# A decoder trunk's opening in a fixed order, its norm weight read from PSUM, and the memory's values ahead of the memory queries

## The chip, the cores and the metric

The kernel runs on one core of a Trainium2 chip. The metric is the device time of one execution in microseconds (us); less is better. Times are compared as medians of repeated runs. One further execution is recorded by the hardware profiler, and all profile lines below come from such executions.

## The reference

The reference computes two layers on a sequence of 512 tokens with 1024 channels, in float32. With `swiglu(t) = (silu(t @ w_gate) * (t @ w_up)) @ w_down`, each layer is

```python
f = swiglu(rmsnorm(h, ffn1_pre_g[l]), ffn1 weights)
h = h + 0.5 * rmsnorm(f, ffn1_post_g[l])
u = rmsnorm(h, mix_pre_g[l])
q_sb, k_sb, v_sb, q_fx, k_fx, v_fx, f_logit, q_mem = split(u @ w_in[l])
o_sb  = stick_breaking_attention(q_sb, k_sb, v_sb)        # 8 heads of 64
o_fx  = forgetting_attention(q_fx, k_fx, v_fx, log_f)     # 8 heads of 64
k_mem, v_mem = split(rmsnorm(mem, mem_norm_g) @ w_mem_kv[l])
o_mem = softmax_attention(q_mem, k_mem, v_mem)            # 4 heads of 128, 256 memory rows
g_sb, g_fx, g_mem = split(sigmoid(u @ w_gate[l] + b_gate[l]))
merged = g_sb * (o_sb @ w_br_sb[l]) + g_fx * (o_fx @ w_br_fox[l]) + g_mem * (o_mem @ w_br_mem[l])
h = h + rmsnorm(merged @ w_out[l], mix_post_g[l])
f = swiglu(rmsnorm(h, ffn2_pre_g[l]), ffn2 weights)
h = h + 0.5 * rmsnorm(f, ffn2_post_g[l])
```

`rmsnorm(t, g)` divides each row by the root of its mean square (plus 1e-6) and multiplies by the weight `g`. The hidden width of `swiglu` is 2816.

## The kernel before

Every float32 matrix is split into a high and a low half in a format that TensorE multiplies in one pass. A product of two matrices is three products of halves: high by high, high by low, low by high (`mm3`, lines 187 to 190). ScalarE makes the high half by a cast (L165, or L168 with a scale), VectorE the low half by subtracting the high one (L166, L169).

The 512 tokens stand in four tiles of 128 rows, `hT[0]` to `hT[3]`. A class `Sub` stands for each norm between two blocks. For one tile it squares and sums the row (`squared`, L520), makes the reciprocal root (`rstd`, L467 to L475), scales the row by it and by the norm's weight (`normed`, L553, into `fs`), transposes the tile on TensorE (`turned`, L563, eight transposes of 128 by 128, into PSUM tiles `ut...`) and splits the result (L168, L169) into `us`. `us[0]` holds channels 0 to 511 and `us[1]` the rest.

Work on TensorE is a queue of jobs, `Q`. A job has weight units, each 128 rows by four or eight, of 512 KB. `fetch` (L236) loads a unit on SyncE's DMA queue into one of two `raw` buffers, and `load` splits it into `wh` and `wl` buffers. `Q.fetch_ahead` issues the next units as soon as a `raw` buffer is counted free. `Q.weave` takes products from the queue one at a time and puts the steps of other chains between them: a chain yields `("wait", us)`, and goes on once that much estimated TensorE time has been recorded. A scheduler underneath may still move an instruction of an engine ahead of others, by its own estimate of when operands are ready; `tc.keep_in_program_order` forbids that for one instruction.

Three places matter here.

*The opening.* `begin()` loads the four tiles of x and the first norm's weight. The weight is one row; `gains(quick=True)` spreads it over 128 partitions by a product with a column of ones (L510, into the PSUM tiles `gqx`) and copies both halves into SBUF (L511). The tiles 0 and 1 are then normed and transposed, and the first two weight units split. These are the units of the first gate tile (`ga`); the first up tile's units (`ua`) are next in the same two `raw` buffers.

*Halves.* In each `ffn` the first gate and up tile are computed for tokens 0 to 255 first and then for tokens 256 to 511 (`halved`), so that the first 96 products need only two tiles. In the opening, tiles 2 and 3 are transposed while the first half runs. Products are issued by `gemm`: one output tile after another, and for each group of 128 channels the three products of halves together. `pga` and `pua` are the gate and up outputs in PSUM of the first block of a layer, `pgc` and `puc` those of its last.

*Entry to the mixing.* While the last tiles of the block before are normed and transposed (`uta`), TensorE works on what doesn't need them: the memory's keys (`pmk`) and the first of two blocks of its values (`pmv_0`). Then come the first block of memory queries (`pqm`, which needs all four tiles), the second block of values, and the second block of queries. The four memory heads follow: scores (`zm`), a softmax on VectorE and ScalarE, transposes (`ptm`), the product with the values (`pvm`), woven with the remaining projections. Between the two, SyncE stores each finished tile of h (`hsave`, L1243), behind which later weight loads on that queue wait.

```python
for c in range(2):
    un = wpair(w_in[l], ND, 3080 + c * 256, f"qm{l}_{c}")
    marks["qm", c] = Q.add(un, lambda c=c, un=un: q_mem(c, un), src.ready(range(NT)) if c == 0 else None)
    if c == 0:
        marks["values"] = rest()
```

`rest()` adds the second block of values. The wait ahead of a tile's transposes is `W_U[t] + self.slack`, with a slack of 4.0 for the norm in front of the mixing.

## Time and profile before

| | |
|---|---|
| median of 3 runs | 2448.37 us (2446.9 to 2449.66) |
| profiled execution, time | 2446.09 us |
| profiled execution, span | 2444.1 us |
| TensorE (PE) busy | 2428.7 us, 99% of the span, 12158 products |
| VectorE (DVE) busy | 1546.0 us, 63% |
| ScalarE (ACT) busy | 1175.3 us, 48% |
| weight and activation loads | 272.20 MB read, 114 GB/s over the span |

A timeline row gives the start, the duration, the engine, the line, the operation, what it writes and reads, the shape and how many instructions were merged into it; in brackets stands the idle time of the engine before it and what ended that. A row of the waits gives the instruction that waited, what it waited for, the total in us, how often, and the longest. A window's row gives its length and then, for each engine shown, busy time and number of instructions, the granted TensorE clock, the share of the DMA engines and GB/s. In a row of grouped instructions stand the busy time and the mean duration in ns. A product's duration reaches past the start of the next one, so the pace is read from the distance between starts.

### The profile page before, as it was taken

What the parts mean: (1) busy time and instruction counts of PE and PEld (TensorE: products, weight loads), DVE (VectorE), ACT (ScalarE), POOL (GpSimd) and SP (SyncE); (2) the same over time, 40 slices, a digit from 0 to 9 for tenths busy, and PEclk for the clock granted to TensorE, in tenths of its full rate; (3) what the DMA queues carried; (4) which work ended last, traced back from release to release, by engine and by line L of the source; (5) the groups of instructions that cost most, each with busy time, mean ns of one, the idle gap of its engine ahead of it and who ended that gap; (6) DMA issues with size and microseconds to landing.
All of it is one profiled execution on the core that took longest, in us unless ns stands there. A gap on an engine that the chain in (4) does not pass through costs nothing.

```text
span 2444.1 us, 30901 instructions
## 1 busy us (share of the span) xinstructions
PE 2428.7 (99%) x12158; PEld 2062.1 (84%) x12158; DVE 1546.0 (63%) x2182; ACT 1175.3 (48%) x1895; POOL 72.6 (3%) x129
## 2 busy tenths in 40 slices
PE   8999999999999999999999999999999999999998
PEld 7888889888888888888888888888888888888887
DVE  4464677677876653656644546876788866445466
ACT  4333365577655543433433333555676655333333
POOL 0000000001110000000000000000011100000000
PEclk9999999999999999999999999999999999999999
DMA  4334344222223433333424343442232243333433
GB/s 138 113 129 129 126 167 147 78 74 74 83 65 114 145 104 108 125 125 128 162 87 131 111 142 133 163 131 70 70 94 71 70 138 129 95 129 104 145 114 129
DMA packets 238597, 280.50 MB, mean 115 GB/s; under 512 B 8666, under 2 KB 188914, under 8 KB 238452
## 3 DMA queue, kind: packets, MB, share of 16 engines
q1 hardware_dynamic: 238356, 278.50, 35.5%
q8 instruction: 95, 1.56, 0.3%
q14 instruction: 50, 0.41, 0.0%
q0 software_dynamic: 96, 0.03, 0.0%
HBM read 272.20 MB, written 6.29 MB: 114 GB/s over the span
## 4 chain that ended last, share of the span: by engine, by line
PE 95%; DVE 2%; ACT 2%; DMA 1%; issue 1%; SPq 0%; DVEq 0%; ACTq 0%
PE pg L188 4%; PE pg L189 4%; PE pg L190 4%; PE pgc L188 3%; PE pga L188 3%; PE pgc L189 3%; PE pga L189 3%; PE puc L188 3%; PE puc L189 3%; PE pgc L190 3%; PE puc L190 3%; PE pga L190 3%; PE pua L188 3%; PE pua L190 3%; PE pua L189 3%; PE pdc L188 3%
## 5 line engine op out<-in xcount | busy, mean ns | idle before, releaser
L188 PE MATMUL pg<-us_a,wh_wg 128*128 128x512 f32 x384 | 150.7, 392 | 0.0
L189 PE MATMUL pg<-us_a,wh_wg 128*128 128x512 f32 x384 | 149.8, 390 | 0.0
L190 PE MATMUL pg<-us_a,wl_wg 128*128 128x512 f32 x384 | 149.6, 390 | 0.0
L190 PE MATMUL puc<-us_b,wl_uc 128*128 128x512 f32 (+1 forms) x384 | 142.5, 371 | 0.0
L189 PE MATMUL puc<-us_b,wh_uc 128*128 128x512 f32 (+1 forms) x384 | 142.5, 371 | 0.0
L188 PE MATMUL puc<-us_b,wh_uc 128*128 128x512 f32 (+1 forms) x384 | 142.4, 372 | 0.0
L188 PE MATMUL pgc<-us_b,wh_gc 128*128 128x512 f32 x320 | 124.5, 389 | 0.0
L189 PE MATMUL pgc<-us_b,wh_gc 128*128 128x512 f32 x320 | 124.5, 389 | 0.0
L190 PE MATMUL pgc<-us_b,wl_gc 128*128 128x512 f32 x320 | 124.5, 389 | 0.0
L166 DVE TENSOR_TENSOR wl_uc<-raw_uc,wh_uc 128x1024 fp32r<-128x1024 f32 x44 | 53.9, 1226 | 107.8 <-ACT wh_uc L165 107.8
L166 DVE TENSOR_TENSOR wl_ua<-raw_ua,wh_ua 128x1024 fp32r<-128x1024 f32 x44 | 53.9, 1226 | 100.8 <-ACT wh_ua L165 100.8
L165 ACT CAST wh_uc<-raw_uc 128x1024 fp32r<-128x1024 f32 x44 | 46.2, 1051 | 92.5 <-PE pgc L189 39.4
L166 DVE TENSOR_TENSOR wl_gc<-raw_gc,wh_gc 128x1024 fp32r<-128x1024 f32 x40 | 48.8, 1224 | 62.7 <-ACT wh_gc L165 62.4
L166 DVE TENSOR_TENSOR wl_ga<-raw_ga,wh_ga 128x1024 fp32r<-128x1024 f32 x40 | 48.8, 1224 | 62.3 <-ACT wh_ga L165 62.1
L165 ACT CAST wh_ua<-raw_ua 128x1024 fp32r<-128x1024 f32 x44 | 46.2, 1050 | 86.2 <-PE pga L189 34.1
L188 PE MATMUL pdc<-wh_dc,ahc 128*128 128x512 f32 x224 | 87.2, 389 | 0.0
L189 PE MATMUL pdc<-wl_dc,ahc 128*128 128x512 f32 x224 | 87.2, 389 | 0.0
L189 PE MATMUL pda<-wl_da,aha 128*128 128x512 f32 x224 | 87.2, 389 | 0.0
L190 PE MATMUL pda<-wh_da,ala 128*128 128x512 f32 x224 | 87.2, 389 | 0.0
L188 PE MATMUL pda<-wh_da,aha 128*128 128x512 f32 x224 | 87.2, 389 | 0.0
L190 PE MATMUL pdc<-wh_dc,alc 128*128 128x512 f32 x224 | 87.1, 389 | 0.0
L190 PEld LDWEIGHTS pg<-us_a,wl_wg 128*128 128x128 f32 x384 | 72.1, 188 | 15.1
(442 smaller groups left out, 7264.3 us busy)
## 6 DMA issues: line engine op xcount, KB each, us to landing
raw_da<-in_ffn_w_down_dram SPq DMA_DIRECT2D x58, 512.0 KB, 3.3
raw_dc<-in_ffn_w_down_dram SPq DMA_DIRECT2D x58, 512.0 KB, 3.2
raw_wg<-in_w_gate_dram SPq DMA_DIRECT2D x48, 512.0 KB, 3.5
raw_ga<-in_ffn_w_gate_dram SPq DMA_DIRECT2D x44, 512.0 KB, 3.6
raw_ua<-in_ffn_w_up_dram SPq DMA_DIRECT2D x44, 512.0 KB, 3.6
raw_gc<-in_ffn_w_gate_dram SPq DMA_DIRECT2D x44, 512.0 KB, 3.6
raw_uc<-in_ffn_w_up_dram SPq DMA_DIRECT2D x44, 512.0 KB, 3.6
raw_wo<-in_w_out_dram SPq DMA_DIRECT2D x24, 512.0 KB, 3.3
```

The costliest lines, as they stand in the source:

```text
L165: both = (nc.scalar.copy(h_ap, src), nc.vector.tensor_tensor(l_ap, src, h_ap.bitcast(F32), ALU.subtract))
L166: nc.vector.tensor_tensor(l_ap, src, h_ap.bitcast(F32), ALU.subtract))
L188: nc.tensor.matmul(pt, lh, rh, start=start, stop=False, skip_group_check=free)
L189: nc.tensor.matmul(pt, lh, rl, start=False, stop=False, skip_group_check=free)
L190: nc.tensor.matmul(pt, ll, rh, start=False, stop=stop, skip_group_check=free)
```

## The change

1. *Opening.* The order of ScalarE's and VectorE's instructions in `begin()` is fixed by dependencies without a semaphore (`in_order`). The spread weight stays in PSUM for the scaling of tiles 0 to 2, which reads it there; ScalarE copies it to SBUF later, for tile 3. Nine products of zeros (`warm`) are put on TensorE, six ahead of the weight's spreading and three between the transposes of tiles 0 and 1. The raw tiles of the first up units come from the pool `v` instead of the two `raw` buffers, and are loaded ahead of the last tile of x. The low halves of tiles 0 and 1 and of the first weights are made after both tiles are scaled. The waits before the transposes of tiles 2 and 3 become 6.5 and 3.2.
2. *Halves.* In every `halved`, the products of high by high of all channels and both output tiles come first, then the products with a low half.
3. *Mixing.* The second block of the memory's values is added to the queue ahead of both blocks of queries, and the slack in front of the mixing becomes 6.0.

```diff
         nc.gpsimd.tensor_scalar(nbfor[:], bfor[:], -1.0, None, ALU.mult)
 
 
+    @contextmanager
+    def in_order(*engines):
+
+        traced = nc.cur_bb.bb.instructions
+        mark = traced[-1]
+        yield
+        traced = nc.cur_bb.bb.instructions
+        at = next(k for k in reversed(range(len(traced))) if traced[k] is mark or traced[k].name == mark.name) + 1
+        nosync = mybir.DependencyInfo(mybir.DependencyClass.NoSync, mybir.DependencyReason.DATA)
+        for e in engines:
+            prev = next((i for i in reversed(traced[:at]) if i.engine == e.engine), None)
+            for i in traced[at:]:
+                if i.engine == e.engine:
+                    if prev is not None:
+                        tc.add_manual_dep(i, prev.name, nosync, reason="in_order")
+                    prev = i
+
     HALVES = (slice(0, S // 2), slice(S // 2, S))
     FULL = slice(0, S)
 
-    def split(h_ap, l_ap, src, scale=None):
+    def split(h_ap, l_ap, src, scale=None, later=False):
 
         if scale is None:
-            both = (nc.scalar.copy(h_ap, src),
-                    nc.vector.tensor_tensor(l_ap, src, h_ap.bitcast(F32), ALU.subtract))
+            both = [nc.scalar.copy(h_ap, src)]
+            make = lambda: nc.vector.tensor_tensor(l_ap, src, h_ap.bitcast(F32), ALU.subtract)
         else:
-            both = (nc.scalar.activation(h_ap, src, AF.Copy, scale=scale),
-                    nc.vector.scalar_tensor_tensor(l_ap, src, scale, h_ap.bitcast(F32), ALU.mult, ALU.subtract))
+            both = [nc.scalar.activation(h_ap, src, AF.Copy, scale=scale)]
+            make = lambda: nc.vector.scalar_tensor_tensor(l_ap, src, scale, h_ap.bitcast(F32), ALU.mult, ALU.subtract)
+        if later:
+            return make
+        both.append(make())
         if Q.pinned:
             for ins in both:
                 tc.keep_in_program_order(ins)
...
 
 
         def __init__(self, src, k0, nk, c0, ncol, name, scale=None):
-            self.tags = ("wh", "wl")
+            self.tags, self.place = ("wh", "wl"), "raw"
             self.src, self.k0, self.nk, self.c0, self.ncol, self.name, self.scale = src, k0, nk, c0, ncol, name, scale
             self.h = self.raw = None
 
...
 
         def ring(self):
 
-            return True
+            return self.place == "raw"
 
         def fetch(self):
             if not self.waits():
                 return
-            Q.fetched += 1
-            self.raw = stile([P, self.nk, self.ncol], "raw", "raw_" + self.name, F32)
+            Q.fetched += self.ring()
+            self.raw = stile([P, self.nk, self.ncol], self.place, "raw_" + self.name, F32)
             nc.sync.dma_start(self.raw[:], self.src[self.k0 * P:(self.k0 + self.nk) * P, self.c0:self.c0 + self.ncol]
                               .rearrange("(k p) c -> p k c", p=P))
 
...
                 return
             self.fetch()
             self.split_from(self.raw[:])
+            self.loaded()
+
+        def loaded(self):
             self.raw = None
-            Q.fetched -= 1
+            if self.ring():
+                Q.fetched -= 1
             Q.fetch_ahead()
 
-        def split_from(self, raw):
+        def split_from(self, raw, **how):
             shape = [P, self.nk, self.ncol]
             if isinstance(self.tags, str):
                 both = stile([P, 2] + shape[1:], self.tags, "w_" + self.name)
...
             else:
                 self.h = stile(shape, self.tags[0], "wh_" + self.name)[:]
                 self.l = stile(shape, self.tags[1], "wl_" + self.name)[:]
-            split(self.h, self.l, raw, scale=self.scale)
+            return split(self.h, self.l, raw, scale=self.scale, **how)
 
     class BlockUnit(Unit):
 
...
                 for row, c in zip(rows, HF):
                     nc.sync.dma_start(row, gain_srcs[i][l:l + 1, c])
                 self.gq = stile([P, D], self.tag, "gq" + self.name, F32)
-                for hf, c in enumerate(HF):
-                    pt = pbank("mm", f"gq{self.name}_{hf}")
-                    nc.tensor.matmul(pt[:], ones, rows[hf], start=True, stop=True)
-                    nc.vector.tensor_copy(self.gq[:, c], pt[:])
+                self.spread = [pbank("mm", f"gq{self.name}_{hf}") for hf in range(2)]
+                for pt, row in zip(self.spread, rows):
+                    tc.keep_in_program_order(nc.tensor.matmul(pt[:], ones, row, start=True, stop=True))
             if self.g_post is not None:
                 self.gp = gain_row(*self.g_post, self.tag, "gp" + self.name)
             if self.g_pre is not None and not quick:
...
                 Q.load_ahead()
                 Q.pinned = False
             c = HALVES[half]
-            for i, pt in enumerate(st["p"]):
-                yield from gemm(pt[:, c], (ug, uu)[i // 2], i % 2, lambda k: act(k, c))
+
+            for uns, pts in ((ug, st["p"][:2]), (uu, st["p"][2:])):
+                for low in (False, True):
+                    for un in uns:
+                        for k, (m, pt) in itertools.product(range(un.nk), enumerate(pts)):
+                            kk, cols = un.k0 + k, slice(m * P, (m + 1) * P)
+                            wh, wl = un.h[:, k, cols], un.l[:, k, cols]
+                            ah, al = act(kk, c)
+                            if low:
+                                nc.tensor.matmul(pt[:, c], wh, al, start=False, stop=False, skip_group_check=True)
+                                nc.tensor.matmul(pt[:, c], wl, ah, start=False, stop=kk == ND - 1, skip_group_check=True)
+                            else:
+                                nc.tensor.matmul(pt[:, c], wh, ah, start=kk == 0, stop=False, skip_group_check=True)
+                            yield (1 + low) * S // 2 * PE_US
             if half == 1:
                 for m in range(2):
                     hidden(f + m, st["p"][m], st["p"][2 + m])
...
             marks["gates", br] = Q.add(ug, lambda: (us_ for m in range(2) for us_ in sigmoid(m)))
             return Q.add(ub, run)
 
+        marks["values"] = rest()
         for c in range(2):
             un = wpair(w_in[l], ND, 3080 + c * 256, f"qm{l}_{c}")
             marks["qm", c] = Q.add(un, lambda c=c, un=un: q_mem(c, un), src.ready(range(NT)) if c == 0 else None)
-            if c == 0:
-                marks["values"] = rest()
         marks["first"] = marks["qm", 0]
 
         heads = [(0, p) for p in range(NP)] + [(1, p) for p in FOX]
...
     kvs = [([], []) for _ in LAYERS]
     subs = [Sub("x", None, (0, 0), False, "k")]
     for l in LAYERS:
-        subs.append(Sub(f"a{l}", (1, l), (2, l), True, "k", 4.0))
+        subs.append(Sub(f"a{l}", (1, l), (2, l), True, "k", 6.0))
         subs.append(Sub(f"b{l}", (3, l), (4, l), False, "v"))
         subs.append(Sub(f"c{l}", (5, l), (0, l + 1) if l < L - 1 else None, True, "k"))
+
+    def warm(n):
+
+        for _ in range(n):
+            tc.keep_in_program_order(nc.tensor.matmul(wps[:], wsb[:, 0:P], wsb[:, 0:S], start=True, stop=True))
 
     def begin():
 
...
         new_h("x")
         Q.hold = True
         nc.sync.dma_start(hT[0][:], x[0, 0:P, :])
+        warm(6)
         sub.gains(quick=True)
         nc.sync.dma_start(hT[1][:], x[0, P:2 * P, :])
-        Q.fetch_ahead()
-        for t in range(2, NT):
-            nc.sync.dma_start(hT[t][:], x[0, t * P:(t + 1) * P, :])
+
+        ug = Q.jobs[0][0]
+        for un in ug[2:]:
+            un.place = "v"
+        for un in ug[:2]:
+            un.fetch()
+        nc.sync.dma_start(hT[2][:], x[0, 2 * P:3 * P, :])
+        for un in ug[2:]:
+            un.fetch()
+        nc.sync.dma_start(hT[3][:], x[0, 3 * P:4 * P, :])
         sub.begin()
-        for t in range(2):
+        sub.alloc()
+        lows = {}
+
+        def turn(t, hf):
+            ts_ = slice(t * P, (t + 1) * P)
+            pt = pbank("z", f"utx_{t}_{hf}")
+            for e in range(4):
+                d = 4 * hf + e
+                nc.tensor.transpose(pt[:, e * P:(e + 1) * P], sub.fs[t][:, d * P:(d + 1) * P], ident[:])
+            lows[t, hf] = split(sub.us[hf][:, :, 0, ts_], sub.us[hf][:, :, 1, ts_],
+                                pt[:].rearrange("p (e q) -> p e q", e=4), scale=RS, later=True)
+
+        def stats(t):
             sub.squared(hT[t][:], sub.sh[t], 0, sub.fs[t][:])
-            sub.normed(t, HF)
-        for t in range(2):
-            sub.turned(t)
-            Q.jobs[0][0][t].load()
-        for t in range(2, NT):
-            sub.squared(hT[t][:], sub.sh[t], 0, sub.fs[t][:])
-            yield ("wait", 2.0)
-            sub.normed(t)
-            yield ("wait", 3.0)
+            return rstd(sub.sh[t], 0)
+
+        def scaled(t, hf, r):
+            nc.vector.scalar_tensor_tensor(sub.fs[t][:, HF[hf]], hT[t][:, HF[hf]], r, sub.spread[hf][:], ALU.mult, ALU.mult)
+
+        with in_order(nc.scalar, nc.vector):
+            r = stats(0)
+            for hf in range(2):
+                scaled(0, hf, r)
+            r = stats(1)
+            for hf in range(2):
+                turn(0, hf)
+            warm(3)
+            low0 = ug[0].split_from(ug[0].raw[:], later=True)
+            for hf in range(2):
+                scaled(1, hf, r)
+            turn(1, 0)
+            turn(1, 1)
+            low1 = ug[1].split_from(ug[1].raw[:], later=True)
+            lows[0, 0]()
+            lows[1, 0]()
+            low0()
+            ug[0].loaded()
+            lows[0, 1]()
+            lows[1, 1]()
+            low1()
+            ug[1].loaded()
+            r = stats(2)
+            for hf in range(2):
+                scaled(2, hf, r)
+            for un in ug[2:]:
+                un.load()
+            for pt, c in zip(sub.spread, HF):
+                nc.scalar.copy(sub.gq[:, c], pt[:])
+            sub.squared(hT[3][:], sub.sh[3], 0, sub.fs[3][:])
+            sub.normed(3)
+        sub.done.update((0, 1))
+        for t, us_ in ((2, 6.5), (3, 3.2)):
+            yield ("wait", us_)
             sub.turned(t)
             yield ("pe", 0.9)
 
...
         Q.until(before["late"])
         Q.weave(None, limit, must)
 
+    wps, wsb = pbank("z", "warm"), tmp("warm").bitcast(BF16)
+    nc.vector.memset(wsb[:, 0:S], 0.0)
     mc = None
     for l in LAYERS:
         i, mn = 3 * l, []
```

More of the change, by code (lines that the diff above doesn't have):

```diff
@@ L1 @@
-import math
-from contextlib import ExitStack
+import itertools
+from contextlib import ExitStack, contextmanager
 import concourse.bass as bass
```

## The prediction

> **What bounds the kernel now.** I read the page first (busy time by engine, the chain that ended last), then the waits of TensorE, then the timeline and the stretches (windows) where those waits lie.
>
> ```profile
> PE 2428.7 (99%) x12158; PEld 2062.1 (84%) x12158; DVE 1546.0 (63%) x2182; ACT 1175.3 (48%) x1895; POOL 72.6 (3%) x129
> ...
> PE 95%; DVE 2%; ACT 2%; DMA 1%; issue 1%; SPq 0%; DVEq 0%; ACTq 0%
> ```
>
> TensorE is busy for 2428.7 of 2444.1 us and makes 95% of the last chain. The change takes no matrix product away, so it can only win idle time of TensorE, some 15 us, or time in which it runs slowly. The waits of TensorE, longest first, say where idle time is:
>
> ```profile
> PE gqx L510 <- DMA grow<-in_ffn_pre_g_dram: 3.9, 1, 3.9
> PE utx L563 <- DVE fx L553: 1.9, 1, 1.9
> PE pgc L188 <- ACT us_b L168: 0.5, 2, 0.2
> PE uta L563 <- DVE nha L468: 0.5, 1, 0.5
> PE pqm L189 <- DVE us_a L169: 0.2, 1, 0.2
> ```
>
> Two waits of the opening (`gqx`, `utx`) are most of it; then come the second halves of the first gate tiles (`pgc`) and the entry to the mixing (`uta`, `pqm`). The change touches these three places and no other. Next, the timeline of the opening:
>
> ```profile
> 0.88 0.17 DVE L503 MEMSET ones<- 1x128 f32 x1
> ...
> 3.86 3.75 PE L510 MATMUL gqx<-grow,ones 1*128 1x512 f32 x4 [3.86 <-DMA grow<-in_ffn_pre_g_dram]
> ...
> 6.09 0.16 DVE L475 SCALAR_TENSOR_TENSOR nhx<-nhx 128x1 f32<-128x1 f32 x1
> 6.17 0.68 DVE L511 COPY gqx<-gqx 128x512 f32<-128x512 f32 x1
> ...
> 6.89 0.75 DVE L553 SCALAR_TENSOR_TENSOR fx<-hx,nhx,gqx 128x512 f32<-128x512 f32 x1
> ...
> 8.06 0.69 DVE L511 COPY gqx<-gqx 128x512 f32<-128x512 f32 x1
> ...
> 8.86 1.23 DVE L166 TENSOR_TENSOR w_ga<-raw_ga,w_ga 128x1024 fp32r<-128x1024 f32 x1
> ...
> 9.40 1.04 ACT L165 CAST w_ga<-raw_ga 128x1024 fp32r<-128x1024 f32 x1
> 10.00 2.07 DVE L553 SCALAR_TENSOR_TENSOR fx<-hx,nhx,gqx 128x512 f32<-128x512 f32 x3
> ...
> 10.80 2.82 PE L563 MATMUL utx<-ident,fx 128*128 128x128 f32 x12 [1.93 <-DVE fx L553]
> ...
> 11.96 0.60 ACT L168 ACTIVATE us_x<-utx 128x512 fp32r<-128x512 f32 x1 [0.36 <-PE utx L563]
> 11.99 1.29 DVE L169 SCALAR_TENSOR_TENSOR us_x<-utx,us_x 128x512 fp32r<-128x512 f32 x2
> ...
> 13.46 0.80 PE L188 MATMUL pga<-us_x,w_ga 128*128 128x256 f32 x2
> ```
>
> TensorE idles until the scaled tiles `fx` come. VectorE is what makes them late: between the rows of `fx` it runs two copies of the gain (L511, 0.68 and 0.69) and a weight's low half (L166, 1.23), so the last of the four pieces ends at 12.07. The first product starts at 13.46, and starts slowly:
>
> ```profile
> 13.46:16.46 3.00, 3.00 (x13) 1.00 0.00 0
> 17.02:20.02 3.00, 3.00 (x28) 1.00 0.80 220
> ```
>
> Both stretches call TensorE fully busy at a granted clock of 1.00, yet the first holds 13 products and the second 28 pieces of work at its edges included: 0.23 us each against 0.12 (29.72 to 29.84 in a later row). The granted clock does not show this; the counts do.
>
> **The change, part by part.** *Opening, order on VectorE and ScalarE.* The two copies leave VectorE (the scaling reads the spread gain from PSUM; the copies go to ScalarE, later) and L166 goes behind the second tile. The PSUM operand is a new form; I price it as the 0.75 of L553, since the two L169 pieces, which read PSUM, take 1.29 together. The first piece of tile 0 follows L475 at 6.3; the second needs the second spread product, ended at 7.61 at the latest (3.86 and 3.75), so it ends between 7.8 and 8.4; then tile 1's three small steps (0.16 for L475, about 0.2 for the others) and two pieces, ending at 9.9 to 10.3 instead of 12.07. On ScalarE, in the new order, two casts of tile 0 (0.60), the first weight (1.04), then tile 1's: the first product starts at about 11.0, and at 12.6 if TensorE is still slow, since then eight transposes take 1.9 (12 in 2.82) and the three extra `warm` products stand before the last eight.
>
> *Pace.* Nine `warm` products of 512 columns run while TensorE would idle: six before the spread products, from about 1.1 (VectorE's memsets, which they follow, end near 1.05), three between the transposes. At the slow pace one is two of 0.23, six take 2.8 and end at 3.9, against 3.86 for the gain row's landing, so they cost nothing; if that cover were gone, each costs 0.46. If they bring the full pace before 11 us, the 13 slow products save 13 x 0.11 = 1.4.
>
> *The 48 gate products of the first half.* All sixteen high ones come first, so neither low half is needed at the start; the second weight's cast ends 1.4 after the first product (0.60 left of tile 1, then 1.04, less overlap) and costs 0.5, as eight products take 1.0. VectorE then makes low halves (four of 0.65, two of 1.23), the last at 15.2; TensorE asks for it only at 15.3. 48 x 0.12 + 0.5 puts the end at 17.3. VectorE, next in line, scales tile 2 until 17.2, so the transposes there find it barely ready: VectorE is what is late next.
>
> *Transfers.*
>
> ```profile
> SPq L236 <- DVE w_ga L166: 8.0, 2, 5.6
> ```
>
> SyncE stood 8.0 us on the weight ring before it could fetch the up weights; now these land in buffers of another pool and are issued at once, ahead of the last tile of x, which is pushed back by two transfers of 512 KB. That tile is wanted at about 18, so I cost the push at nothing; without that cover TensorE waits for it one for one.
>
> *End of the opening.* 17.3, then 1.04 for transposes, 48 x 0.12 for the up products, 1.04 for the last transposes:
>
> ```profile
> 27.49 1.04 PE L563 MATMUL utx<-ident,fx 128*128 128x128 f32 x8
> 28.78 0.51 PE L188 MATMUL pga<-us_x,w_ga 128*128 128x256 f32 x2 [0.25 <-ACT us_x L168]
> ...
> 29.72 0.28 PE L190 MATMUL pga<-us_x,w_ga 128*128 128x256 f32 x1
> 29.84 0.28 PE L188 MATMUL pga<-us_x,w_ga 128*128 128x256 f32 x1
> ```
>
> The second half starts at 25.2 instead of 28.78, and its first six products, which take 1.06 (28.78 to 29.84) instead of 0.72, lose 0.3 less, since four up products now stand after the transposes in the built order. That is 3.9. With 0.3 off for hand-overs that such a sum forgets I take **3.6**. At the slow pace the sixteen high products run from 12.6 to 16.3 (0.23 each), the other 32 to 20.1, and the second half starts at 28.0: 1.1 is left.
>
> *The three other second halves.* At 887.34 the same six products take 1.06:
>
> ```profile
> 887.34 0.50 PE L188 MATMUL pgc<-us_b,w_gc 128*128 128x256 f32 x2 [0.25 <-ACT us_b L168]
> ...
> 888.40 0.28 PE L188 MATMUL pgc<-us_b,w_gc 128*128 128x256 f32 x1
> ```
>
> The wait for the cast stays (no work is put before it here), but the low halves are wanted only after sixteen products; up to 0.34 goes in each. I take **0.8** for three (0 to 1.0).
>
> *Entry to the mixing, twice.*
>
> ```profile
> 384.08 0.28 PE L874 MATMUL pmv<-wh_mv,mn 128*128 128x256 f32 x1
> 384.84 1.06 PE L563 MATMUL uta<-ident,fa 128*128 128x128 f32 x8 [0.48 <-DVE nha L468]
> ...
> 391.86 0.27 PE L873 MATMUL pmv<-wl_mv,mn 128*128 128x256 f32 x1
> 392.27 0.50 PE L189 MATMUL pqm<-us_a,wh_qm 128*128 128x512 f32 x1
> 392.61 0.39 PE L190 MATMUL pqm<-us_a,wl_qm 128*128 128x512 f32 x1
> 392.84 0.40 PE L188 MATMUL pqm<-us_a,wh_qm 128*128 128x512 f32 x1
> ```
> ```profile
> 1602.85 0.27 PE L873 MATMUL pmv<-wl_mv,mn 128*128 128x256 f32 x1
> 1603.33 0.50 PE L189 MATMUL pqm<-us_a,wh_qm 128*128 128x512 f32 x1 [0.20 <-DVE us_a L169]
> ```
>
> Layer 0 loses 0.64 (0.76 between starts instead of 0.12), 0.29 and 0.11 (0.34 instead of the 0.23 that follows); layer 1 0.36 and about 0.1. With 2.0 more slack the transposes of tile 2 stand behind twelve more products (1.44), and 48 value products stand between the last transposes and the queries. Both stalls go: **1.5** (0 to 1.5). What is late next are the values' weights: on SyncE they now stand behind the store of the last tile, ahead of the query weights.
>
> ```profile
> 386.46 1.28 DVE L553 SCALAR_TENSOR_TENSOR fa<-hx,nha,gqa 128x1024 f32<-128x1024 f32 x1
> ...
> 388.26 1.22 DVE L166 TENSOR_TENSOR wl_qm<-raw_qm,wh_qm 128x1024 fp32r<-128x1024 f32 x1
> ```
>
> The query weights that held those places before were both split by 389.48; the values are wanted from about 390.8, and the last tile (387.74) is transposed only after that split. So the cover is some 1.3 us; beyond it each us is paid twice, once in each layer.
>
> **Sum:** 3.6 + 0.8 + 1.5 = 5.9. The profiled run took 2446.09 (span 2444.1 and 2.0 around it), so 2440.2 for its like. Its time lies 2.28 under the median of the runs, 2448.37; from the median it is **2442.5**.
>
> **The rivals.** *The pace stays slow in the opening.* For it: 3.75 us of spread products and 2.82 of transposes went by and 13 products after them were still slow. If neither kind counts, the six `warm` products are 2.8 us, less than the 3.0 us of real products that it took before. Opening 1.1, sum 3.4, 2445.0. Against: the new opening is busy almost without a break from 1.1 on.
>
> [...]
>
> *A new wait at the mixing.* The values' weights come after their turn; 0.75 to 1.5 per layer takes back the 1.5 and somewhat more: 2444 to 2446. Against it stand the 1.3 us above.
>
> *Slower: the heads run dry.* Before, the second block of values filled the softmax of the first memory head:
>
> ```profile
> L874 PE MATMUL pmv<-wh_mv,mn 128*128 128x256 f32 x16 | 4.5, 283 | 0.0
> ```
>
> with its two sister groups 46 products, 46 x 0.12 = 5.5 us. Used up earlier, they leave 5.5 uncovered in each layer if nothing takes their place: 11.0 less 4.4 won elsewhere, 2455. It decides where the work between a head's scores and its transposes falls below 5.5. Against it: in the built order thirty query products (0.23) and twelve scores (0.12) now stand there, 8.3 us, as long as before (46 and 12 of 0.12, six of 0.23); they come from the projections, of which enough are left.
>
> *Nothing happens* (the waits removed are hidden by others): 2448. The instruction orders of the built program are as the change says, which leaves little for it.
>
> **How the numbers follow.** Forecast 0.60 (2442.5, its own range 2440.0 to 2444), slow pace 0.22, new wait 0.10, slower 0.06, nothing 0.02. Measurement of this kernel can tell about 0.2% from no change, 4.9 us: faster means under 2443.5. The forecast lies mostly there (0.55 of its 0.60), with 0.05 from the next two: 0.60 faster, 0.34 within, 0.06 slower. The range, 2440.0 to 2446.5, takes in the slow pace and most of the new wait and leaves out the slower case.
>
> **What would show it.** The first `pga` product near 11.0 with 0.12 between starts, and the second half at about 25.2; a first product after 12.5 with 0.2 or more between starts means the slow pace. No L511 copies on VectorE; the last piece of tile 1 by 10.3. No `uta` wait and no gap before `pqm` near 390 and 1600; `pmv` waiting on VectorE there means the new wait; `ptm` waiting means the dry heads. The forecast is wrong if the opening saves under 2.5 us or any of these waits exceeds 1 us.

## The result and the profile after

| | before | after |
|---|---|---|
| median | 2448.32 us (12 runs, 2446.9 to 2450.66) | 2443.08 us (12 runs, 2441.49 to 2444.39) |
| ratio, 95% interval | | 0.9977 (0.9969 to 0.9984) |
| profiled execution, time and span | 2446.09, 2444.1 us | 2443.11, 2441.3 us |

The change makes the kernel 5.2 us faster, 0.23%. The two profiled executions are only 3.0 apart; where the other 2.2 lie is one of the questions below. The waits of TensorE, after:

```profile
PE warm L1354 <- DVE warm L1438: 1.2, 1, 1.2
PE pts L946 <- ACT ts L979: 1.1, 1, 1.1
PE pgc L651 <- ACT us_b L185: 0.5, 2, 0.2
PE pga L651 <- ACT w_ga L182: 0.4, 1, 0.4
PE mt L862 <- DVE fa L726: 0.4, 1, 0.4
```

The waits of `gqx` (3.9), `utx` (1.9), `uta` (0.5) and `pqm` (0.2) are gone. New are one of the `warm` products for their zeros at the very start (1.2), one for the second weight's cast in the opening (`w_ga`), and two far from the edited places: `mt` (transposes of the memory rows, at 334 us) and `pts` (transposes in the stick-breaking heads, at 628 us).

The timeline of the opening, after (start, duration, engine, line, operation):

```profile
1.25 2.74 PE L1354 MATMUL warm<-warm 128*128 128x512 bf16 x6 [1.25 <-DVE warm L1438]
4.03 3.75 PE L534 MATMUL gqx<-grow,ones 1*128 1x512 f32 x4
6.35 0.75 DVE L1393 SCALAR_TENSOR_TENSOR fx<-hx,nhx,gqx 128x512 f32<-128x512 f32 x1
7.70 2.03 PE L1384 MATMUL utx<-ident,fx 128*128 128x128 f32 x8
7.81 0.75 DVE L1393 SCALAR_TENSOR_TENSOR fx<-hx,nhx,gqx 128x512 f32<-128x512 f32 x1 [0.72 <-PE gqx L534]
9.17 1.41 DVE L1393 SCALAR_TENSOR_TENSOR fx<-hx,nhx,gqx 128x512 f32<-128x512 f32 x2
9.52 1.49 PE L1354 MATMUL warm<-warm 128*128 128x512 bf16 x3
10.80 1.92 PE L1384 MATMUL utx<-ident,fx 128*128 128x128 f32 x8
12.55 1.39 PE L651 MATMUL pga<-us_x,w_ga 128*128 128x256 f32 x8
13.25 1.04 ACT L182 CAST w_ga<-raw_ga 128x1024 fp32r<-128x1024 f32 x1
14.34 1.22 PE L651 MATMUL pga<-us_x,w_ga 128*128 128x256 f32 x8 [0.41 <-ACT w_ga L182]
15.47 1.21 DVE L183 TENSOR_TENSOR w_ga<-raw_ga,w_ga 128x1024 fp32r<-128x1024 f32 x1
17.31 1.41 DVE L1393 SCALAR_TENSOR_TENSOR fx<-hx,nhx,gqx 128x512 f32<-128x512 f32 x2
19.24 1.03 PE L586 MATMUL utx<-ident,fx 128*128 128x128 f32 x8
26.73 1.64 PE L651 MATMUL pga<-us_x,w_ga 128*128 128x256 f32 x12
```

The last piece of tile 1 is scaled at 10.58 (9.17 and 1.41), not at 12.07. But TensorE is slow right up to the first product: spreading 3.75, sixteen transposes 2.03 and 1.92, just as before. The first product comes at 12.55, and full pace right behind it: from 12.93 on the products start 0.11 to 0.13 apart. After eight of them TensorE stands until the second weight's cast ends at 14.29. The second half starts at 26.73 instead of 28.78.

The second half at 885 us, and the entry to the mixing, both TensorE's timeline after:

```profile
885.40 2.17 PE L651 MATMUL pgc<-us_b,w_gc 128*128 128x256 f32 x16 [0.25 <-ACT us_b L185]
887.41 0.28 PE L648 MATMUL pgc<-us_b,w_gc 128*128 128x256 f32 x1
```
```profile
383.61 1.04 PE L586 MATMUL uta<-ident,fa 128*128 128x128 f32 x8
387.36 1.03 PE L586 MATMUL uta<-ident,fa 128*128 128x128 f32 x8
```

Sixteen high products take 2.01 (885.40 to 887.41), 0.11 over 16 x 0.1185; before, the first six alone lost 0.34. The transposes of the mixing wait for nothing, and there is no gap ahead of the queries.

Where the time went can be followed by one marker. The first `mt` stands behind 300 us of weight products without a wait, so its start carries what the opening cost and nothing else (TensorE's timeline, before and after):

```profile
335.00 0.49 PE L827 MATMUL mt<-ident,mraw 128*128 128x128 f32 x3
```
```profile
332.66 1.03 PE L862 MATMUL mt<-ident,mraw 128*128 128x128 f32 x8
```

The opening won 2.34. From the marker to the end of the last product, at 2436.78 and 2433.90, the rest took 2101.78 and 2101.24, only 0.54 less, although the entries to the mixing won 1.1 and 0.5 by the same comparison of starts (2.01 ahead at 337 us, 3.11 at 432; 2.37 at 1590, 2.84 at 1643), and the three other second halves 0.24, 0.26 and 0.25 (near 885, 1239 and 2096 us). The waits of `mt`, `pts` and one of `utc` at 1233, 0.6, 1.3 and 0.4 in distances between starts, took most of it back.

### The profile page after: what moved, and what is told of

Its sections match the earlier page's. It is cut to its first block, busy times and chain, and to the rows that moved or that the text cites. A ratio compares the mean times of both kernels' runs of the same rounds, so it can differ in the third digit from the quotient of the medians.

```text
span 2441.3 us, 30918 instructions
## 1 busy us (share of the span) xinstructions
PE 2429.5 (100%) x12167; PEld 2062.0 (84%) x12167; DVE 1544.3 (63%) x2182; ACT 1173.4 (48%) x1897; POOL 72.6 (3%) x129
## 4 chain that ended last, share of the span: by engine, by line
PE 94%; DVE 2%; ACT 2%; DMA 1%; issue 1%; DVEq 0%; ACTq 0%
PE pg L208 4%; PE pg L210 4%; PE pg L209 4%; PE pgc L208 3%; PE pgc L210 3%; PE pgc L209 3%; PE puc L208 3%; PE puc L209 3%; PE puc L210 3%; PE pga L208 3%; PE pga L210 3%; PE pua L210 3%; PE pga L209 3%; PE pda L209 3%; PE pua L209 3%; PE pda L208 3%
## 5 line engine op out<-in xcount | busy, mean ns | idle before, releaser
L210 PE MATMUL puc<-us_b,wl_uc 128*128 128x512 f32 x320 | 124.5, 389 | 0.0
L208 PE MATMUL puc<-us_b,wh_uc 128*128 128x512 f32 x320 | 124.5, 389 | 0.0
L209 PE MATMUL puc<-us_b,wh_uc 128*128 128x512 f32 x320 | 124.5, 389 | 0.0
```

What stands on the lines that cost most here:

```text
L208: nc.tensor.matmul(pt, lh, rh, start=start, stop=False, skip_group_check=free)
L209: nc.tensor.matmul(pt, lh, rl, start=False, stop=False, skip_group_check=free)
L210: nc.tensor.matmul(pt, ll, rh, start=False, stop=stop, skip_group_check=free)
```

## The experiments

### The three parts alone, and the changed kernel once more

Each edit was put by itself into the kernel before; the opening's edit includes the new order of products in the first block, where its low halves come late.

```diff
 # open_only: begin(), gains() and split() as after; halves: the new order in the first block only
+            if name != "a0":  <old order>   else:  <new order>
 # halves_only: begin() as before; the new order in the other blocks
+            if name == "a0":  <old order>   else:  <new order>
 # mix_only: begin() and halves as before
+        marks["values"] = rest()          # ahead of both blocks of queries
-        subs.append(Sub(f"a{l}", (1, l), (2, l), True, "k", 4.0))
+        subs.append(Sub(f"a{l}", (1, l), (2, l), True, "k", 6.0))
```

> The opening alone: the new begin() with its fixed order, warm products, PSUM scaling and early up weights, and the high products first in the first block only; the other blocks' halves, the order of the values and the slack as before. Theory (from the trace after): the opening is worth 2.6 us, a median of 0.9989 of before, with the second half at about 26.7. Rival 1 (the prediction's sum): 3.6. Rival 2: the opening is worth only about 1, since what it wins is lost again at the waits near 333 and 630 us that the trace after shows; then these waits appear here too.

> The high products first in the three other blocks that are computed in halves, all else as before. Theory: 0.6 us (0.2 each; the wait of 0.5 for the cast stays, and the two later losses near 0.17 each go), median 0.9998 of before. The prediction's term was 0.8. Rival: nothing in the median, because VectorE's low halves are only asked for earlier by the second output tile; then the products after the cast still show steps of 0.23 or more.

> The values ahead of both blocks of queries and the slack of 6.0, all else as before. Theory: 1.1 us in layer 0 and 0.8 in layer 1, together 1.9, median 0.9992 of before; no wait of the transposes or the first queries near 390 and 1600 us. The prediction's term was 1.5. Rival: the wait of 1.1 us near 630 us (transposes of the stick-breaking heads in layer 0) comes from this edit, since it moves work ahead of the heads; then it is here as well, and the gain is under 1.

> The changed kernel once more, unchanged, beside the three parts. Theory: the waits near 333, 630 and 1233 us, 2.1 us together, are those of one execution: at least two of the three are gone or moved in this profile, and its span is 2439 to 2441.5. The median is 5.2 under before, the sum of the three parts within 0.7. Rival: the waits recur at the same places, and belong to the change.

| | median, runs | ratio to before, 95% | first `mt` | rest from there |
|---|---|---|---|---|
| before | 2450.51, 32 | | 335.00 | 2101.8 |
| open_only | 2448.91, 11 | 0.9992 (0.9983 to 1.0001) | 333.00 | 2108.0 |
| halves_only | 2449.63, 11 | 0.9996 (0.9987 to 1.0005) | 335.93 | 2105.9 |
| mix_only | 2446.88, 11 | 0.9987 (0.9978 to 0.9995) | 335.38 | 2101.8 |
| after_again | 2444.85, 10 | 0.9979 (0.9970 to 0.9988) | 332.69 | 2102.9 |

(The last two columns are from one execution of each; the first row has the profile of before that the prediction used.)

The medians of the parts fall by 1.6, 0.9 and 3.6, together 6.1, against 5.7 for the whole on the same chip: the parts add up, and the largest in the medians is the mixing. Each alone is known to some 2 us only, and the mixing's interval alone leaves out no gain at all. The theory of 2.6 for the opening and 1.9 for the mixing lies inside the intervals, and so does the prediction's 3.6 for the opening. So does the second rival's 1 for the opening, and its sign came: the waits at `mt` and `pts` stand in open_only too, at 335 and 632 us.

```profile
PE mt L866 <- DVE fa L730: 1.2, 1, 1.2
PE pts L950 <- ACT ts L983: 1.1, 1, 1.1
```

By starts open_only is 2.01 ahead of before at the marker, 0.85 at 340 us, 0.25 at 400 and 1.2 behind at 632.

The last column bears on the gap between profiles and medians. Three executions have the old entry to the mixing, and their rests are 2101.8, 2108.0 and 2105.9: the profiled execution of before is the shortest of them by 4. Some of that goes with the chip or the hour of these runs: there the median of before is 2.2 longer than beside the result, and after_again's rest is 1.7 longer than that of after, which is the same kernel. But the profile of before was a lucky execution by its time alone, as its 2446.09 lies below all twelve runs of before in the result (2446.9 to 2450.66). Its opening was lucky too, in a smaller way. Four executions with the old opening (halves_only, mix_only and the two below) start their first product at 14.70 to 15.10, not 13.46. VectorE's and ScalarE's timeline in halves_only, and TensorE's, show why:

```profile
7.27 1.06 ACT L544 ACTIVATE fx<-hx 128x1024 f32<-128x1024 f32 x1 [1.26 <-DMA hx<-in_x_dram]
10.51 1.23 DVE L183 TENSOR_TENSOR w_ga<-raw_ga,w_ga 128x1024 fp32r<-128x1024 f32 x1 [0.60 <-ACT w_ga L182]
11.65 0.75 DVE L577 SCALAR_TENSOR_TENSOR fx<-hx,nhx,gqx 128x512 f32<-128x512 f32 x1
12.45 2.82 PE L587 MATMUL utx<-ident,fx 128*128 128x128 f32 x12 [3.37 <-DVE fx L577]
```

The second tile of x landed 1.1 later than in the profile of before (7.25 against 6.16), the first weight 1.7 later, and VectorE, whose order put the weight's low half ahead of `fx`, waited for it. The new order has no such step, so with x's second tile at 6.72, 7.49 and 7.95 its first product stays at 12.55, 12.59 and 12.83. The marker's mean is 335.48 in five executions with the old opening and 332.78 in three with the new one: 2.7.

The waits of after are not a fixed price of the change. In after_again, which is the same kernel, there is none at 334 us and the `pts` wait is 0.2, while that of `utc` at 1233 is back and longer (0.6 instead of 0.2), and others stand beside it:

```profile
PE pwo L209 <- DVE wl_wo L183: 1.6, 3, 0.6
```

Its span of 2443.0 is also above the 2439 to 2441.5 expected. But the waits don't belong to the execution alone. Nine profiles have the new opening (these three and six below). In six of them `mt` waits 0.4 to 1.2 at this place, and in five `pts` waits 0.6 to 1.2; in the five profiles with the old opening `mt` has no wait there of 0.1 or more, and `pts` 0.2 at most. So with the new opening these waits come more often, and they take part of its gain back. That TensorE arrives earlier isn't the whole reason: pace_row (below) has both waits, 1.1 and 1.2, and its marker, 337.87, is later than that of before. What the reason is wasn't tested.

The wait at `pts` could be followed to its root, since after and no_warm (below) run in step from 335 to 560 us, with a difference of 0.00 on TensorE. SyncE's, ScalarE's and TensorE's timeline, after and then no_warm:

```profile
582.86 0.37 SPq L256 DMA_DIRECT2D raw_wb<-in_w_br_mem_dram  x1
588.81 1.05 ACT L182 CAST wh_wb<-raw_wb 128x1024 fp32r<-128x1024 f32 x1 [1.18 <-DMA raw_wb<-in_w_br_mem_dram]
628.47 1.31 PE L946 MATMUL pts<-ident,ts 128*128 128x128 f32 x10 [1.13 <-ACT ts L979]
```
```profile
582.86 0.37 SPq L256 DMA_DIRECT2D raw_wb<-in_w_br_mem_dram  x1
587.63 1.05 ACT L182 CAST wh_wb<-raw_wb 128x1024 fp32r<-128x1024 f32 x1
627.28 1.31 PE L946 MATMUL pts<-ident,ts 128*128 128x128 f32 x10
```

The same load, issued at the same moment, landed 1.2 later; ScalarE and VectorE stayed 1.19 behind for 40 us, and TensorE met it at the next transposes that they feed. From issue to landing this load took 4.7 to 4.9 us in the five profiles with the old opening and 4.7 to 6.5 in the nine with the new one (5.9 in after, 6.2 in open_only, 6.5 in pace_row, the three that wait over 1 us at `pts`). The waits of `pwo` for the output weights' low half are of the same kind; that their loads came late was not traced.

### What opens TensorE's full pace

In the openings seen so far full pace began after stretches that were largely transposes (in halves_only 2.65 of the 3.6 us from 12.45 on), against the prediction's reading ("If neither kind counts", in its rival of the slow pace). Four kernels put one kind of work in place of the six `warm` products. Each ran once, and only the pace in its trace is read; the tile of zeros is twice as wide in them, so the work begins at 1.51 (at 2.60 with the transposes, which wait for the identity).

```diff
-        warm(6)
+        probe(n)      # n times, in program order:
 # pace_zeros,   n = 20:  matmul(wps[:], wsb[:, 0:P], wsb[:, 0:S])          bf16 zeros, 128 rows
 # pace_turns,   n = 40:  transpose(wps[:, 0:P], ident[:], ident[:])        float32
 # pace_row,     n = 5:   matmul(wps[:], wt[0:1, 0:P], wt[0:1, :])          float32 zeros, one row
 # pace_rows128, n = 5:   matmul(wps[:], wt[:, 0:P], wt[:, :])              float32 zeros, 128 rows
```

> The changed kernel with twenty warm products of zeros instead of six ahead of the gain's spreading (8.5 us at the slow pace of 0.427 each, which delays everything behind them). It asks what opens the full pace. [...] Rival: products of zeros do not count, and all twenty stand at 0.43.

> The same with forty transposes of the identity matrix (0.213 each at the slow pace) in place of the six warm products. [...] Rival (the prediction's reading): transposes do not count, and all forty stand at 0.213.

> The same with five float32 products of one row by 512 columns (two passes of 0.853 each) in place of the six warm products, the shape of the gain's spreading. Theory: one-row products do not count as busy, all ten passes stand at 0.853, and the spreading after them too, 12 us in all without full pace; this is why the changed kernel's spreading and six warm products together, 6.5 us of unbroken work, opened nothing by 7.8 us. [...]

> The same as the one-row case, but with all 128 rows (of zeros). [...] Rival: what does not count is float32, and all ten passes stand at 0.853.

TensorE's timeline, one row of each kernel (a float32 product is two passes, ten rows for five products), then two stretches of pace_turns' transposes (length, busy time of PE with its count, of PEld, of DVE, clock, DMA share, GB/s):

```profile
1.51 6.26 PE L1359 MATMUL warm<-warm 128*128 128x512 bf16 x20 [1.51 <-DVE warm L1444]
```
```profile
2.60 6.43 PE L1359 MATMUL warm<-ident 128*128 128x128 f32 x40 [2.60 <-POOL ident masks.py:199]
```
```profile
1.51 8.90 PE L1359 MATMUL warm<-warm 1*128 1x512 f32 x10 [1.51 <-DVE warm L1444]
10.21 3.62 PE L534 MATMUL gqx<-grow,ones 1*128 1x512 f32 x4
```
```profile
1.51 7.10 PE L1359 MATMUL warm<-warm 128*128 128x512 f32 x10 [1.51 <-DVE warm L1444]
8.53 1.98 PE L534 MATMUL gqx<-grow,ones 1*128 1x512 f32 x4
```
```profile
2.70:5.90 3.20, 3.20 (x16) 3.20 (x17) 0.00 (x0) 1.00 0.82 260
6.50:8.80 2.30, 2.30 (x23) 2.29 (x21) 0.00 (x0) 1.00 1.01 332
```

Work counts, as the expectations put it, if it brings full pace on. Transposes count: 0.213 between starts for the first seventeen, 0.109 from 6.4 us on. Products of zeros count: 0.427 to 0.216 at about 5.1. Float32 with 128 rows counts: 0.853 to 0.430 at about 6.7. One row does not: all ten passes stand at 0.853, and the spreading behind them still takes 3.62, fourteen passes in 12 us of unbroken work, where pace_rows128 spreads in 1.98. In pace_row full pace comes at 16.8 only, 3.1 us after the transposes behind the spreading begin. pace_row went as its theory said, and the rivals of the other three, by which all stands at the slow pace, did not hold.

The moment varies in these traces: from the start of unbroken work that counts to full pace it took 3.1 to 5.8 us (13.75 to 16.8 in pace_row, 2.60 to 6.4 in pace_turns, 10.80 to 16.6 before). In open_only full pace came 3.3 us after the first `warm` product (1.24 to 4.5), the last 0.5 of it one-row work; in after, after_again and cast_on_dve (below) the same six products at the same time brought nothing before the spreading ended. What sets the moment was not shown.

### The mixing's two edits apart, and the opening without and with other covers

```diff
 # slack_only: mix_only without the move of the values (slack 6.0)
 # values_only: mix_only with the slack at 4.0
 # no_warm: the changed kernel
-        warm(6)
-            warm(3)
 # cast_on_dve: the changed kernel
-            warm(3)
+            warm(1)
-            low1 = ug[1].split_from(ug[1].raw[:], later=True)
             lows[0, 0]()
+            low1 = ug[1].split_from(ug[1].raw[:], later=True, copy=nc.vector.tensor_copy)
```

> The slack of 6.0 in front of the mixing alone; the order of the values, the opening and the halves as before. Theory: it takes away the waits of the transposes for VectorE near 385 and 1596 us, which were 0.65, 1.46 and 0.85 in layer 0 and 0, 1.0 and 0 in layer 1 of three executions: 1.3 us in the mean; the stop of 0.3 to 0.5 ahead of the first query products stays in both layers. Rival: the transposes that come later push the queries back, whose wait grows by what was won.

> The values ahead of both blocks of queries alone, with the slack of 4.0; the opening and the halves as before. Theory: the stop ahead of the first query products (0.30 to 0.49 in layer 0, 0.36 to 0.83 in layer 1) goes, 1.0 us for both; the waits of the transposes near 385 and 1596 us stay. Together with the slack 2.3, against 3.6 (1.2 to 5.4) measured for both edits together. Rival: the values carry most of the gain, because the transposes' wait is for a split of the query weights that now comes later; then the transposes' wait is gone too.

> The changed kernel without its nine warm products. [...] Rival: warm products matter for nothing else than filling; the first product is earlier and so is the second half, by 0.4.

> The changed kernel with the second weight's high half cast on VectorE, which stands idle for 0.9 to 1.35 us there, instead of ScalarE, and one warm product instead of three between the two tiles' transposes. Theory: the wait of 0.6 to 0.7 after the first eight products goes, the first product is at 11.9 to 12.1, the last low half at 16.6 as before, so the end of the first 48 products is set by VectorE: tile 2 is transposed 0.3 to 0.6 us earlier, and as much is won in all (0.9998 of the changed kernel). Rival: full pace comes later, as the break before the first product is longer; then the first 16 products take 3.4 instead of 1.9 and it is slower by up to 1.2.

| | median, runs | ratio to before (2449.63, 29 runs), 95% | first `mt` |
|---|---|---|---|
| slack_only | 2448.13, 11 | 0.9993 (0.9985 to 1.0002) | 335.76 |
| values_only | 2447.91, 11 | 0.9992 (0.9983 to 1.0001) | 335.31 |
| no_warm | 2441.97, 7 | 0.9972 (0.9961 to 0.9983) | 333.27 |
| cast_on_dve | 2445.58, 11 | 0.9982 (0.9973 to 0.9991) | 332.05 |

In the medians the mixing's edits win 1.5 and 1.7, about the same, and add up to the 3.6 within what can be told; neither interval leaves out no gain. TensorE's timeline at the entry, values_only and then slack_only:

```profile
385.39 1.06 PE L587 MATMUL uta<-ident,fa 128*128 128x128 f32 x8 [1.17 <-DVE nha L492]
```
```profile
391.32 0.73 PE L208 MATMUL pqm<-us_a,wh_qm 128*128 128x512 f32 x2
392.04 0.50 PE L209 MATMUL pqm<-us_a,wh_qm 128*128 128x512 f32 x1
392.38 0.40 PE L210 MATMUL pqm<-us_a,wl_qm 128*128 128x512 f32 x1
```

With the values alone the transposes still wait, with the slack alone the first queries still stop (four of them take 1.29, from 391.32 to the next start at 392.61, 0.4 more than at 0.23 each). In these two traces each edit takes the one wait it is near, and neither rival holds.

In no_warm the pace came at about 15.8, 3 us later than after (TensorE's timeline):

```profile
10.81 1.94 PE L1383 MATMUL utx<-ident,fx 128*128 128x128 f32 x8 [0.92 <-DVE fx L1392]
12.58 3.61 PE L651 MATMUL pga<-us_x,w_ga 128*128 128x256 f32 x16
```

The first sixteen products take 3.45 (12.58 to 16.03), but the second weight's cast holds them up for 0.1 only, and the marker moves by 0.6 only (333.27). Two microseconds behind the marker even that is gone. From the thirteenth `mt` product on, both stand at the same moment (TensorE's weight loads, after and then no_warm):

```profile
334.69 0.42 PEld L862 LDWEIGHTS mt<-ident,mraw 128*128 128x128 f32 x4 [0.17 <-DVE fa L726]
```
```profile
334.69 0.42 PEld L862 LDWEIGHTS mt<-ident,mraw 128*128 128x128 f32 x4 [0.18 <-DVE fa L726]
```

VectorE's `fa`, which they wait for, starts at 333.36 in both, and ahead of it stands a weight whose cast waited for its landing until 331.13 in both. The 0.6 won in the opening only made TensorE wait for it. The first product of no_warm came at 12.58, not earlier than 12.55 as its rival has it, since x's second tile landed 1.0 later than in after. The median of no_warm is no worse than that of the changed kernel, rather better (0.9972 against 0.9979 and 0.9977, intervals overlapping); that nine products of zeros cost or win anything in the whole isn't shown.

cast_on_dve did in the opening what was expected, except that the first product came at 12.34 and not at 11.9 to 12.1. VectorE's and TensorE's timeline:

```profile
11.60 0.68 DVE L182 CAST w_ga<-raw_ga 128x1024 fp32r<-128x1024 f32 x1
12.34 2.62 PE L651 MATMUL pga<-us_x,w_ga 128*128 128x256 f32 x16
```

The wait after eight products is gone, the marker is at 332.05, 0.6 ahead of the changed kernel. The time doesn't show it: 0.9982. On the same chip its eleven runs (2443.06 to 2449.0) lie 3.6 above the seven of no_warm (2441.55 to 2443.47) in the median, although its marker is 1.2 earlier. Its profile, with a rest of 2104.3, holds 1.3 us of `mt` waits, 1.6 of `utc` and 0.6 of `pwo`; that of no_warm has none of these. So an earlier marker alone is no gain in the whole. Why these waits come in one kernel and not in the other wasn't tested.

## Why the prediction came out as it did

*The time.* 2442.5 was forecast and 2443.08 measured, with a sum of 5.9 against 5.24. That the sum is so close is in part luck. In the pair of profiles the edited places won 4.7 (2.34, 0.75 and 1.6) and the time fell by 3.0, since the waits at `mt`, `pts` and `utc`, for which the sum has no term, took most of the rest; in the medians the opening won less than its term and the mixing more, each known to some 2 us.

*Opening, forecast 3.6, measured 2.34 in the pair and 2.7 between the means at the marker, 1.6 (-0.2 to 4.2) in the medians of open_only.* By its own bound of 2.5 the pair counts as a miss. The order on VectorE and ScalarE went as worked out: no copies of the gain, `fx` with a PSUM operand at 0.75 as priced, tile 1 done at 10.58 (forecast 9.9 to 10.3, with x's tile 0.6 later), and the `warm` products ended at 3.98 against 4.03 for the spreading, at no cost. The step that failed is the pace. "If they bring the full pace before 11 us": in after they did not, as the spreading uses one row, which does not count (14 passes, 12 us without full pace in pace_row), and takes up the 3.75 us that follow them. In open_only they did, at 4.5, but it was lost again by 7.7, so that the first product still came at 12.83. In after full pace came at about 12.9, behind transposes and the three later `warm` products. So the slow-pace line for the first product (12.6) was right and the sixteen slow products after it were not: the truth lies between 3.6 and 1.1. The prediction's "If neither kind counts" held for the one-row spreading but not for the transposes, which count (0.213 to 0.109 after 3.8 us in pace_turns); what it saw, full pace 3.0 us after the first product, was the end of a stretch that began with the transposes at 10.80, 5.8 us before it. The wait for the second weight was forecast at 0.5 and is 0.57.

*What is late next.* VectorE, as forecast, but later: the last low half ends at 16.68 and not at 15.2, since ScalarE's casts of tile 1 end at 12.50 and 13.35 and the low halves follow them. Tile 2 is scaled at 18.72, 0.5 ahead of its transposes at 19.24. The last tile of x, pushed back, cost nothing: no wait for it is in the profile.

*Second halves, forecast 0.8.* The pair shows 0.24 at 885, 0.26 at 1239 and 0.25 at 2096 us (2.63 ahead before it, 2.88 behind it), 0.75 together, as forecast (up to 0.34 each). In the medians 0.9, with an interval from -1.2 to 3.2.

*Entry to the mixing, forecast 1.5 in a range of 0 to 1.5.* The pair shows 1.1 in layer 0 and 0.5 in layer 1, together 1.6, against 1.04 and 0.46 read from the rows: for the execution that it was read from, the term was right. (Another 0.3 in layer 1 lies ahead of it, at the memory rows' transposes near 1547 us.) The medians show 3.6 (1.2 to 5.4), which 1.5 still fits. What was too small is the upper end of the range, because it was read from one execution: the waits of the transposes there were 0.65 in layer 0 and none in layer 1, and in two other executions with that entry they lost 1.46 and 1.0, and 0.85 and 0. A bound from one lucky row was taken for the largest gain. The new wait on the values did not come, nor did the heads run dry: no `pmv` or `ptm` stands among the waits.

*From the median.* Taking the sum from the median and not from the profiled run was the right choice, and it matters here: that run was 2.3 under the median, and its own rows can understate what is won.

## What to carry to other kernels

Before you price a stall from one profiled execution, look at the same place in another: waits that hang on a load's landing differed here by more than a microsecond between executions (one load of 512 KB took 4.7 to 6.5 us), and an edit that gives them slack is worth its mean, not what one row shows. If a filler is to bring TensorE to full pace, look at how many rows it and the work behind it use: in the probes work on 128 rows brought it 3.6 to 5.2 us after its start and one-row work not in 12 us, and a filler of 2.7 us in front of a one-row product was lost in after, after_again and cast_on_dve, and in open_only what it brought was lost again. And follow a gain by markers behind each stage: one shows what a stage won, the next what is left of it. Here up to 1.2 us won in the opening was gone again at the next wait for a weight load.

## What the runs showed of the hardware

- Float32 products of one row by 512 columns stayed at 0.853 a pass for 14 passes, 12 us (pace_row); with 128 rows of zeros the passes fall to 0.430 after 5.2 us (pace_rows128). Where full pace had been opened by other work, one-row passes ran at 0.43 too (pace_zeros, 1.98 for four passes against 3.62 in pace_row).
- Transposes opened full pace like products of zeros: 0.213 to 0.109 after 3.8 us (pace_turns), 0.427 to 0.216 after 3.6 (pace_zeros). Full pace was also lost again: in open_only the spreading ran at full pace from about 4.5 (2.22 for four passes), TensorE stood 1.12 us, and the transposes fell back from 0.11 to 0.21 at 7.7. Ahead of 7.7 lie 2.2 us of one-row passes and the 1.12 of standing still, and the runs don't tell how much of either it takes; in pace_zeros full pace outlasted 2.0 us of one-row passes. The rows of open_only, TensorE's timeline:

```profile
3.99 2.22 PE L534 MATMUL gqx<-grow,ones 1*128 1x512 f32 x4
7.33 1.67 PE L1389 MATMUL utx<-ident,fx 128*128 128x128 f32 x8 [1.12 <-DVE fx L1398]
8.79 1.49 PE L1359 MATMUL warm<-warm 128*128 128x512 bf16 x3
```

- The granted clock is given as 1.00 from the start of each of these traces, at the slow pace too, so that it does not show when full pace first comes. Where full pace was lost, in open_only, it is given as 0.50 in every whole microsecond from 8 to 14, and as 1.00 again from 15 on (0.998 in the mean of that execution, 0.999 or 1.0 in the other thirteen).
- VectorE cast a 128x1024 weight in 0.68 (cast_on_dve, at 11.60); the same cast took ScalarE 1.04 (after, at 13.25).
- The same 512 KB load, issued at 582.86 in two executions, landed at 588.7 and 587.6; in all fourteen profiles it took 4.7 to 6.5 us.
